# Sums of squares per head: one fp32 matmul against two rounded passes, in a hybrid attention / DeltaNet layer

## The chip, the core and the metric

The kernel runs on one core of one Trainium2 chip. The metric is the device time in microseconds of one execution. TensorE (PE) multiplies, VectorE (DVE) and ScalarE (ACT) do the elementwise work, GpSimd (POOL) clears a few tiles and issues some DMAs, SyncE (SP) issues most DMAs.

## The reference

One layer over 512 latent tokens and 256 context tokens of width 1024. Two mixers run side by side: windowed attention with normalised queries and keys, and a gated DeltaNet whose queries and keys are normalised too. Their outputs are gated, projected and added; a squared-ReLU MLP follows. What matters here are the two normalisations, both over the 64 features of one head:

```python
def rms_norm(x, g):
    xf = x.astype(jnp.float32)
    return xf * lax.rsqrt(jnp.mean(xf * xf, axis=-1, keepdims=True) + EPS) * g.astype(jnp.float32)

def l2_normalize(x):
    return x * lax.rsqrt(jnp.sum(x * x, axis=-1, keepdims=True) + EPS)
...
q_a = axial_rope(rms_norm(heads(aq, ATTN_Q_HEADS), q_norm_g), row, col)
k_a = axial_rope(rms_norm(heads(ak, ATTN_KV_HEADS), k_norm_g), row, col)
k_ac = rms_norm(heads(cak, ATTN_KV_HEADS), k_norm_g)
...
q_d = l2_normalize(heads(q_d, DN_HEADS)) * DN_HEAD_DIM ** -0.5
k_d = l2_normalize(heads(k_d, DN_HEADS))
```

## The kernel before, in words

Features lie on partitions and tokens on columns, so one tile of 128 partitions holds two heads. A sum over the 64 features of a head is a sum over 64 partitions. The kernel takes it on PE: `bones` is a 128x128 matrix of ones in two diagonal blocks of 64, and `bones` times the squares gives on each partition the sum of its own head.

The large projections are not run in plain fp32. A value is split into an upper part `hi` (ACT rounds it to the short format fp32r, L224) and a rest `lo` (DVE subtracts, L225), and `mm3` (L331, L333, L335) adds the products upper-upper, upper-rest and rest-upper in the same PSUM bank. Weights are split in the same manner (`wh` on ACT, L295; `wl` on DVE, L300, or by a DMA that GpSimd issues, L297 and L298). The sums of squares are the exception: `bones` and the squares are plain fp32 and go in one matmul call, which the trace shows as two MATMUL records.

There are 13 such sums of 512 columns and 5 of 256:

- `qk_norm` (the matmul is L566): attention keys, 512 latent columns and 256 context columns; four tiles of attention queries, 512 columns each. ACT squares the projection (L563) and copies it with its gain (L564), PE sums, DVE rotates (L569 to L572), ACT takes Ln and Exp of the sums (L185, the line of a helper), DVE multiplies (L577).
- `l2n` (L781): four tiles of DeltaNet keys, 512 and 256 columns each (in the order of the program just before `chunk_mats`); four tiles of DeltaNet queries of 512 columns, beside the first steps of the scan. ACT squares (L778), PE sums, ACT takes Ln and Exp, DVE multiplies (L786, L788).

A further matmul with `bones` (L861) sums decays and is of 96 columns.

Around these sums the program goes on as follows. `chunk_mats` builds the decay matrices (L913 to L939), `invert` solves triangular systems on DVE in a long row of small dependent steps (L972, L973), first for the context, later for the latent chunks. `back` (L983) transposes the results, `combine` (L993 to L1004) and the scan steps (`chain_step`, L1243 to L1322) use them on PE. Attention runs between (`scores`, reduction on DVE at L681; `outputs`, L725 to L747). Projections of gates (L1148, L1194) are work for PE that nothing waits for at once.

Buffers in SBUF come from a ring of 167 units of 256 columns (`Arena`): `alloc` takes the next free place behind the last one, `free` gives it back; large tiles that stay are taken from the far end. `NSKIP` moves the ring's pointer on at one place, by as many turns of `alloc(1024).free()`, four units each.

The order of instructions on each engine is not the order of the program. A planner (`Lists.run`) gives each instruction a cost and a latency, and lets each engine take the ready instruction of lowest rank. Ranks are positions in the program, moved by the table `SHIFTS` (an engine or all, a first and an end position, so many places). The order it finds is fixed in the program that runs.

Of the kernel before, what the change touches and what calls it, by code (L numbers as in the profile page):

```python
# [10 lines left out]
F32 = mybir.dt.float32  # L11
F32R = mybir.dt.float32r
BF16 = mybir.dt.bfloat16
AF = mybir.ActivationFunctionType
# [20 lines left out]
NPL = ()  # L35
WEARLY = 0
STICK = 50
NSKIP = 2
WARM = (0, 3, 3, 3, 2, 0, 0, 0)
NROWS = 2  # L40
ND1 = 3
# [1 line left out]
P = 128  # L43
# [74 lines left out]
def tile_layer(ctx: ExitStack, tc: tile.TileContext, I: dict, out: bass.AP, dbg=None):  # L118
    nc = tc.nc
    V, A, G, PE = nc.vector, nc.scalar, nc.gpsimd, nc.tensor  # L120
# [5 lines left out]
    mats = ctx.enter_context(tc.tile_pool(name="mats", bufs=1))  # L126
# [16 lines left out]
    alloc, bank = mem.get, lambda n=1: banks.get(n * 512)  # L143
# [3 lines left out]
    def load(out, key, *at):  # L147
        d = nc.sync.dma_start(out=out, in_=I[key][at] if at else I[key])
        if lastload:
            tie(d.ins, lastload[0].ins.name)  # L150
        return d

    def cload(key, shape, pool=const):
        t = pool.tile(list(shape), F32, name=f"c_{key}")
        load(t, key)
        return t
# [5 lines left out]
    r32 = lambda ap: ap.bitcast(F32R)  # L162
# [14 lines left out]
    def act(out_, in_, func, **kw):  # L177

        sets = TABLES.get(func)
        if sets and actg["set"] not in sets:  # L180
            head = A.preload_act_table_set(sets[0])
            for o in actg["ops"]:
                tie(head.ins, o.name)
            actg.update(set=sets[0], head=head.ins, ops=[head.ins])
        r = A.activation(out_, in_, func, **kw)  # L185
        if sets:
            tie(r.ins, actg["head"].name)
            actg["ops"].append(r.ins)
        return r
# [255 lines left out]


    ident = cload("ident", [P, P], mats)
    bones = cload("bones", [P, P], mats)
    identb = mats.tile([P, P], BF16, name="identb")
    V.tensor_copy(identb, ident)  # L450
    maskb = mats.tile([P, 2, P], BF16, name="maskb")
# [3 lines left out]
    mt.free()  # L455
    cs = alloc(1024, True)
    cost, sint = cs[:, :512], cs[:, 512:]
    load(cost, "cost")
    load(sint, "sint")
    selq = cload("selq", [64, 80])  # L460
# [37 lines left out]

    for _ in range(NSKIP):
        alloc(1024).free()  # L500
# [55 lines left out]
                return e.value  # L556


    def qk_norm(acc, n, gain, turn=False):

        t = alloc(1024)
        raw, sq = t[:, :n], t[:, 512:512 + n]
        A.activation(sq, acc, AF.Square)  # L563
        A.activation(raw, acc, AF.Copy, scale=gain)  # L564
        ss = bank()
        PE.matmul(ss[:, :n], bones, sq, start=True, stop=True)  # L566
        if turn:
            rot = alloc(512)
            V.stream_shuffle(rot.ap, raw, [(i + 16) % 32 for i in range(32)])  # L569
            V.tensor_tensor(raw, raw, cost, op=ALU.mult)  # L570
            V.tensor_tensor(rot.ap, rot.ap, sint, op=ALU.mult)
            V.tensor_tensor(raw, raw, rot.ap, op=ALU.add)  # L572
            rot.free()
        act(sq, ss[:, :n], AF.Ln, bias=epsc, scale=1.0 / HD)
        ss.free()
        act(sq, sq, AF.Exp, scale=-0.5)
        V.tensor_tensor(raw, raw, sq, op=ALU.mult)  # L577
        return t
# [13 lines left out]
    def k_attn():  # L592

        acc = yield from in_tile_steps(T_AK, True)
        t = qk_norm(acc[:, :512], SEQ, kg, True)
        t2 = qk_norm(acc[:, 512:768], CTX, kg)
        acc.free()
        for src, o in ((t[:, :512], slice(0, 512)), (t2[:, :CTX], slice(512, 768))):
            for kv, r in enumerate(own):
                for r2 in own:  # L600
                    A.activation(r32(KH[kv][r2, o]), src[r], AF.Copy)
                V.tensor_tensor(r32(KLo[kv][r, o]), src[r], KH[kv][r, o], op=ALU.subtract)
        t.free()
        t2.free()
        yield
# [19 lines left out]
    def q_attn(j):  # L625
        acc = yield from in_tile_steps(T_AQ + j, False)
        t = qk_norm(acc.ap, SEQ, qgs, True)
        acc.free()
        src = t[:, :512].rearrange("p (b t) -> p b t", b=4)
        for kv, r in enumerate(own):  # L630
            split(src[r], Q[kv][r, :, j, :], Q[kv][own[1 - kv], :, j, :])
        t.free()
        yield
# [140 lines left out]
    def l2n(y, scale, parts, eps):  # L774

        n = parts[-1][1]
        t = alloc(n)
        A.activation(t.ap, y, AF.Square)  # L778
        for lo, hi in parts:
            ss = bank()  # L780
            PE.matmul(ss[:, :hi - lo], bones, t[:, lo:hi], start=True, stop=True)  # L781
            act(t[:, lo:hi], ss[:, :hi - lo], AF.Ln, bias=eps)
            ss.free()
        act(t.ap, t.ap, AF.Exp, scale=-0.5)
        if scale == 1.0:
            V.tensor_tensor(y, y, t.ap, op=ALU.mult)  # L786
        else:
            V.scalar_tensor_tensor(y, y, scale, t.ap, op0=ALU.mult, op1=ALU.mult)  # L788
        t.free()
# [10 lines left out]
    t, t2 = alloc(TOK), alloc(TOK)  # L800
# [249 lines left out]
    def mats():  # L1050
        for q in range(4):
            l2n(kT[q].ap, 1.0, ((0, SEQ), (SEQ, TOK)), epsc)
            yield
        for gi in range(3):
            yield from chunk_mats(gi)
# [282 lines left out]
    def rest():  # L1338
        for q in range(4):
            l2n(qT[q].ap, HD ** -0.5, ((0, SEQ),), epsc4)  # L1340
            yield
        for g in (1, 2):
            to_tokens(VTM, vT, g)
            yield
        for t in vT:
            t.free()
        for g in (1, 2):
            to_tokens(KTM, kT, g)
            yield
# [30 lines left out]
    for g in range(2):  # L1380
# [20 lines left out]
        for a in range(2):  # L1401
            lo, hi = quad(a, 0), quad(a, 1)
# [38 lines left out]
    for qq in range(2):  # L1441
# [3 lines left out]
        for a in range(2):  # L1445
            n = 2 * qq + a
            t = alloc(512)
# [304 lines left out]
class Step:  # L1752
# [39 lines left out]
    def cost(self):  # L1792

        n = self.cols
        if self.kind == "InstMatmult":
            if self.dtype.endswith("32r"):
                return (226 if n == 512 else max(60, 7 + .44 * n)), n * .44 + 175
            if self.dtype.endswith("16"):
                return 96, 240
            if self.whole:  # L1800
                return (110, 280) if self.ins.is_transpose else (max(62, 1.72 * n), max(62, 1.72 * n) + 170)
            return (142, 300) if self.tile[0] == P else (30 if self.tile[1] > HC else 19, 220)
        if self.kind == "InstStreamTranspose":
            return 1950, 2090
        if self.eng == "DVE":
            own = 67 + 1.04 * n + 60 * self.psum if n > 8 else 100
            return own, own + 85
        if self.eng == "Activation":
            own = 1290 if "Load" in self.kind else max(195, 36 + .893 * n) + 20 * self.psum
            return own, own + 130  # L1810
        return 550, 560


# [67 lines left out]
class Lists:  # L1881
# [114 lines left out]


SHIFTS = (
# [12 lines left out]
)  # L2011


# [120 lines left out]
```

## Time and profile before

| what | us |
|---|---|
| median of 3 runs | 871.12 (870.12 to 871.73) |
| profiled execution, its own time | 871.5 |
| its span in the trace | 869.7 |
| PE busy | 852.3 |
| DVE busy | 647.0 |
| ACT busy | 498.4 |

The span is the time from the first to the last instruction in the trace; 1.8 us of the profiled execution's time lie around it. Busy is time in which at least one instruction of the engine is under way. The granted clock of PE is full in every slice.

### The profile page before, as it was taken

What the parts mean: (1) busy time and instruction counts of PE and PEld (TensorE: products, weight loads), DVE (VectorE), ACT (ScalarE), POOL (GpSimd) and SP (SyncE); (2) the same over time, 40 slices, a digit from 0 to 9 for tenths busy, and PEclk for the clock granted to TensorE, in tenths of its full rate; (3) what the DMA queues carried; (4) which work ended last, traced back from release to release, by engine and by line L of the source; (5) the groups of instructions that cost most, each with busy time, mean ns of one, the idle gap of its engine ahead of it and who ended that gap; (6) DMA issues with size and microseconds to landing.
All of it is one profiled execution on the core that took longest, in us unless ns stands there. A gap on an engine that the chain in (4) does not pass through costs nothing.

```text
span 869.7 us, 17973 instructions
## 1 busy us (share of the span) xinstructions
PE 852.3 (98%) x7544; PEld 712.8 (82%) x7544; DVE 647.0 (74%) x1113; ACT 498.4 (57%) x882; POOL 26.1 (3%) x42
## 2 busy tenths in 40 slices
PE   9999999999999999899999999999999999999998
PEld 6688778877777778677778899888998899889986
DVE  4865899987779997867848969993876478648741
ACT  5567875487669886587754435552555256415620
POOL 0000001010000002000000000000000000000000
PEclk9999999999999999999999999999999999999999
DMA  9924465533121236733116744743412332342031
GB/s 365 352 72 98 88 134 122 120 76 70 38 38 31 68 131 212 243 99 100 40 54 220 264 144 131 249 139 121 146 33 74 122 140 70 97 128 92 26 121 49
DMA packets 31986, 106.86 MB, mean 123 GB/s; under 512 B 4001, under 2 KB 4513, under 8 KB 31905
## 3 DMA queue, kind: packets, MB, share of 16 engines
q1 hardware_dynamic: 29600, 97.33, 33.6%
q0 software_dynamic: 2304, 8.39, 6.2%
q8 instruction: 59, 0.97, 0.5%
q14 instruction: 23, 0.18, 0.1%
HBM read 103.61 MB, written 2.10 MB: 122 GB/s over the span
## 4 chain that ended last, share of the span: by engine, by line
PE 77%; DVE 9%; ACT 6%; DMA 6%; issue 2%; SPq 0%; ACTq 0%; DVEq 0%
PE banks L331 14%; PE banks L333 14%; PE banks L335 14%; PE banks L1612 14%; PE banks L1148 7%; DMA m<-in_wada 3%; PE banks L1243 3%; PE banks L1194 3%; ACT m L185 2%; PE banks L725 1%; DVE wl L300 1%; DMA wr<-in_win 1%; PE banks L781 1%; DVE m L511 1%; DMA wr<-in_wbr 1%
## 5 line engine op out<-in xcount | busy, mean ns | idle before, releaser
L331 PE MATMUL banks<-m,wh 128*128 128x512 f32 (+1 forms) x568 | 210.7, 374 | 2.2 <-ACT m L224 1.3
L333 PE MATMUL banks<-m,wh 128*128 128x512 f32 (+1 forms) x568 | 211.2, 372 | 0.0
L335 PE MATMUL banks<-m,wl 128*128 128x512 f32 (+1 forms) x568 | 209.9, 370 | 0.1
L295 ACT ACTIVATE wh<-wr 128x1024 fp32r<-128x1024 f32 (+1 forms) x92 | 90.4, 984 | 128.3 <-PE banks L333 82.7
L331 PEld LDWEIGHTS banks<-m,wh 128*128 128x128 f32 x568 | 107.0, 189 | 20.4 <-ACT m L224 1.5
L1612 PEld LDWEIGHTS banks<-m,m 128*128 128x128 f32 x1008 | 122.2, 192 | 0.7
L335 PEld LDWEIGHTS banks<-m,wl 128*128 128x128 f32 x568 | 106.9, 188 | 19.2 <-issue 1.0
L1612 PE MATMUL banks<-m,m 128*128 128x256 f32 x1008 | 122.4, 283 | 0.0
L333 PEld LDWEIGHTS banks<-m,wh 128*128 128x128 f32 x568 | 107.1, 188 | 18.1 <-issue 0.7
L224 ACT ACTIVATE m<-m 128x512 fp32r<-128x512 f32 (+2 forms) x118 | 82.4, 721 | 66.1 <-PE banks L1612 14.9
L1148 PE MATMUL banks<-m,wh 128*128 128x512 f32 x320 | 104.1, 402 | 1.8 <-ACT m L185 1.0
L225 DVE TENSOR_TENSOR m<-m,m 128x512 fp32r<-128x512 f32 (+2 forms) x118 | 92.3, 804 | 15.5 <-ACT m L224 13.9
L300 DVE TENSOR_TENSOR wl<-wr,wh 128x1024 fp32r<-128x1024 f32 (+1 forms) x76 | 84.3, 1109 | 17.1 <-ACT wh L295 14.6
L1739 DVE SCALAR_TENSOR_TENSOR m<-banks,modT,m 128x512 f32<-128x512 f32 x32 | 24.0, 749 | 65.0 <-PE banks L335 64.9
L1148 PEld LDWEIGHTS banks<-m,wh 128*128 128x128 f32 x320 | 58.6, 188 | 14.4 <-ACT m L185 1.4
L1148 PE MATMUL banks<-m,wl 128*128 128x512 f32 x160 | 63.7, 400 | 0.4 <-DVE wl L300 0.4
L331 PE MATMUL banks<-m,m 128*128 128x256 f32 (+1 forms) x136 | 45.5, 340 | 0.4 <-ACT m L295 0.3
L333 PE MATMUL banks<-m,m 128*128 128x256 f32 (+1 forms) x136 | 45.6, 342 | 0.1
L511 DVE SCALAR_TENSOR_TENSOR m<-m,m 128x1024 f32<-128x1024 f32 x32 | 39.1, 1222 | 8.4 <-DMA m<-in_wada 8.2
L335 PE MATMUL banks<-m,m 128*128 128x256 f32 (+1 forms) x120 | 40.2, 337 | 0.0
L1243 PEld LDWEIGHTS banks<-m,m 64*64 64x64 f32 x1600 | 26.7, 134 | 12.5 <-issue 4.3
L1148 PEld LDWEIGHTS banks<-m,wl 128*128 128x128 f32 x160 | 30.0, 188 | 7.3 <-DVE wl L300 1.1
(263 smaller groups left out, 1313.7 us busy)
## 6 DMA issues: line engine op xcount, KB each, us to landing
m<-in_wada SPq DMA_DIRECT2D x48, 512.0 KB, 4.8
wr<-in_wm SPq DMA_DIRECT2D x40, 512.0 KB, 3.6
wr<-in_win SPq DMA_DIRECT2D x38, 512.0 KB, 3.7
m<-in_wm SPq DMA_DIRECT2D x24, 512.0 KB, 3.7
wl<-in_win POOLq DMA_DIRECT2D x16, 512.0 KB, 5.8
m<-in_xT SPq DMA_DIRECT2D x8, 512.0 KB, 5.9
wr<-in_wbr SPq DMA_DIRECT2D x16, 256.0 KB, 2.7
wr<-in_wout SPq DMA_DIRECT2D x8, 512.0 KB, 4.4
```

The lines of the kernel that those rows point to most:

```text
L224: A.activation(r32(hi), src, AF.Copy)
L225: (eng or V).tensor_tensor(r32(lo), src, hi, op=ALU.subtract)
L295: upper[0] = A.activation(r32(hi), raw, AF.Copy)
L300: V.tensor_tensor(r32(lo), raw, hi, op=ALU.subtract)
L331: PE.matmul(acc, w[0][:, k, :], xhi, start=(start and i == 0), stop=False)
L333: r = PE.matmul(acc, w[0][:, k, :], xlo, start=False, stop=(end and w[1] is None))
L335: r = PE.matmul(acc, w[1][:, k, :], xhi, start=False, stop=end)
L511: r = V.scalar_tensor_tensor(wa.ap, wa.ap, 0.5, scr_[0].ap, op0=ALU.mult, op1=ALU.mult, accum_out=modT[:, grp, j:j + 1])
L1148: PE.matmul(acc.ap, w[x][:, k, :], hx[k][y], start=(k == p == 0), stop=(k == KT - 1 and p == 2))
L1194: PE.matmul(pa.ap, w[x][:, j, :], r32(Q[y][:, :, j, :]), start=(j == p == 0), stop=(j == 3 and p == 2))
L1243: runs[n].append(PE.matmul(out_, w, x, start=True, stop=True).ins.name)
L1612: PE.matmul(dst, r32(self.w[w][i][:, k * P:(k + 1) * P]), xs7[x][k][j], start=(n == 0), stop=(n == 11))
```

## The change

Three things change.

1. Each of the 18 sums of squares goes in two passes. A new helper takes two buffers from the ring, lets ACT round the squares into the first and DVE subtract them into the second (`split`), and adds two fp32r matmuls with `bones` in one bank. `bones` itself is loaded into a buffer of the ring and copied into its place by ACT, so that it is marked as rounded; it holds only ones and zeros. The sum of the decays (L861) stays in fp32.
2. The ring's pointer is moved by seven turns in place of two.
3. `SHIFTS` is another table, of 69 entries in place of 60. The planner also gets a cost for a subtraction on GpSimd, which is not used: `POOLS` is False, and the subtraction is on DVE.

```diff
-NSKIP = 2
+NSKIP = 7
+POOLS = False
...
-    bones = cload("bones", [P, P], mats)
+    bones = mats.tile([P, P], F32, name="bones")
+    bt = alloc(256)
+    load(bt[:, :P], "bones")
+    A.activation(r32(bones), bt[:, :P], AF.Copy)
+    bt.free()
+    SPLITTER = G if POOLS else V
...
+    def ones_sum(dst, sq):
+
+        n = sq.shape[-1]
+        hi, lo = alloc(n), alloc(n)
+        split(sq, hi.ap, lo.ap, SPLITTER)
+        PE.matmul(dst, r32(bones), r32(hi.ap), start=True, stop=False)
+        PE.matmul(dst, r32(bones), r32(lo.ap), start=False, stop=True)
+        hi.free()
+        lo.free()
+
     def qk_norm(acc, n, gain, turn=False):
...
-        PE.matmul(ss[:, :n], bones, sq, start=True, stop=True)
+        ones_sum(ss[:, :n], sq)
...
-            PE.matmul(ss[:, :hi - lo], bones, t[:, lo:hi], start=True, stop=True)
+            ones_sum(ss[:, :hi - lo], t[:, lo:hi])
...
+        if self.kind == "InstTensorTensor":
+            return 100 + 2.2 * n, 200 + 2.2 * n
         return 550, 560
...
 SHIFTS = (
-    (0, 2729, 2759, -37), (0, 7350, 8025, -10), (-1, 4917, 4924, 10), (0, 1436, 2436, 180), (-1, 5117, 5177, 30),
...
+    (0, 5262, 5282, 10), (4, 85, 205, 80), (0, 2465, 2615, -30), (2, 7546, 7946, 1000), (2, 6238, 6638, -200),
...
 )
```

24 rows, old and new, of the table SHIFTS are left out of this document.

## The prediction

> **What bounds the kernel now.** I read the page first: the busy times and the chain of work that ended last.
>
> ```profile
> span 869.7 us, 17973 instructions
> PE 852.3 (98%) x7544; PEld 712.8 (82%) x7544; DVE 647.0 (74%) x1113; ACT 498.4 (57%) x882; POOL 26.1 (3%) x42
> ...
> PE 77%; DVE 9%; ACT 6%; DMA 6%; issue 2%; SPq 0%; ACTq 0%; DVEq 0%
> ```
>
> PE is busy for 852.3 of 869.7 us and idle for 17.4 us in all, and 77% of the last chain are its instructions. What shortens PE's work shortens the run, as long as the rest of the order keeps PE fed. An average over the whole says nothing of the places where the sums stand, so I asked next for the busy time by stretches (start and end, length, then busy time and count for each engine, granted clock, DMA share, GB/s). The sums run from 74 to 131 us (keys of both mixers, attention queries) and from 283 to 298 us (DeltaNet queries).
>
> ```profile
> 66.00:99.00 33.00, 20.79 (x41) 1.00 0.42 88
> ...
> 99.00:189.00 90.00, 88.42 (x754) 71.19 (x752) 85.99 (x165) 55.88 (x92) 9.87 (x13) 1.00 0.54 115
> 189.00:281.00 92.00, 88.36 (x689) 70.24 (x688) 72.89 (x131) 69.87 (x127) 3.46 (x4) 1.00 0.22 47
> 281.00:335.00 54.00, 54.00 (x681) 41.08 (x679) 52.66 (x94) 47.95 (x106) 2.07 (x4) 1.00 0.33 103
> 335.00:380.00 45.00, 41.73 (x844) 32.90 (x842) 33.72 (x59) 27.74 (x53) 6.24 (x12) 1.00 0.61 207
> ```
>
> The first line is DVE alone; in the others the columns after the length are PE, weight load, DVE, ACT, POOL. Two things are to be seen. PE is idle for 1.6, 3.6, 0.0 and 3.3 us in the four later stretches, 8.5 us together. And DVE, which is to get 18 new subtractions, is free for 12.2 of 33 us between 66 and 99 and for 19.1 of 92 us between 189 and 281, but full from 99 to 189 (4.0 of 90 us free) and from 281 to 335 (1.3 of 54 us free). Both engines are full where two thirds of the sums stand: the change moves work from one to the other.
>
> **What PE saves.** The chain of waits gives the pitch of matmuls on PE, since there each piece lasts from one release to the next (start, length, what).
>
> ```profile
> 69.57 0.12 PE banks L333
> ...
> 70.04 0.23 PE banks L333
> ...
> 74.00 1.29 PE banks L781 x4
> ...
> 122.52 0.87 PE banks L566 x2
> ...
> 130.33 0.86 PE banks L566 x2
> ```
>
> An fp32r matmul of 512 columns takes 0.23 us of PE, one of 256 takes 0.12. A key tile's two fp32 sums, 512 and 256 columns, take 1.29 us in four records; a sum of 512 columns alone takes 0.86. In two passes these become 2 x 0.23 + 2 x 0.12 = 0.70 and 2 x 0.23 = 0.46 us. The savings are 0.59 us for each of five key tiles (one of attention, four of DeltaNet) and 0.40 us for each of eight query tiles: 2.95 + 3.20 = 6.2 us (6.15 before rounding). The number of weight loads stays at two for each sum.
>
> The Trainium skill (FP8 and Floating Point Precision, TensorE Precision Notes) has a true fp32 product as four passes through the array. By that a sum of 512 columns would cost 0.92 us, not the 0.86 of the row, and the saving would come out near 7.1 us; I keep the row.
>
> **What is added on DVE and ACT.** Subtractions and rounding copies of this form stand in the trace already (mean ns of one before the second bar); for their pitch I take neighbours on a full DVE (start, length).
>
> ```profile
> L225 DVE TENSOR_TENSOR m<-m,m 128x512 fp32r<-128x512 f32 x84 | 56.3, 687 | 9.7 <-ACT m L224 8.3 <-PE banks L1612 0.8
> ...
> 108.38 0.69 DVE L572 TENSOR_TENSOR m<-m,m 128x512 f32<-128x512 f32 x1
> 108.98 0.69 DVE L929 TENSOR_TENSOR m<-m,m 128x512 f32<-128x512 f32 x1
> ...
> 361.53 0.42 DVE L1395 TENSOR_TENSOR m<-m,banks 128x256 f32<-128x256 f32 x1
> 361.86 0.69 DVE L1153 SCALAR_TENSOR_TENSOR m<-m,m 128x512 f32<-128x512 f32 x1
> ```
>
> ```profile
> L224 ACT ACTIVATE m<-m 128x512 fp32r<-128x512 f32 x84 | 51.7, 627 | 57.3 <-PE banks L1612 14.9 <-DMA m<-in_wm 13.4 <-DVE m L1470 6.4
> ```
>
> On DVE a subtraction of 512 columns costs 0.60 us from start to start and one of 256 columns 0.33 us: 13 x 0.60 + 5 x 0.33 = 9.5 us in all. Of these the DeltaNet keys take 4 x 0.93 = 3.7 us, the attention keys and queries 0.93 + 4 x 0.60 = 3.3 us, the DeltaNet queries 4 x 0.60 = 2.4 us. On ACT a rounding copy of 512 columns lasts 0.63 us, and one of 256 is bounded by the same, so the 18 copies are at most 18 x 0.63 = 11.3 us.
>
> What hides them: for the DeltaNet keys, the 12.2 us in which DVE is free between 66 and 99 us; they cost nothing, and 3.7 us on DVE's queue if that cover is gone. ACT is busy for 57% of the whole span, for 55.9 of 90 us in the first full stretch of DVE and for 48.0 of 54 us in the second; there four more copies (2.5 us) still fit into its 6 us. I cost ACT at nothing but the wait below. The subtractions of the attention tiles (3.3 us) and of the DeltaNet queries (2.4 us) lie in the two full stretches and have no cover there. They push back what stands behind them on DVE. What that is in the second stretch is seen in its order of time:
>
> ```profile
> 320.66 0.21 DVE L973 TENSOR_TENSOR m<-m,m 128x60 f32<-128x60 f32 x1
> ...
> 321.36 2.02 DVE L983 STREAM_TRANSPOSE m<-m 128x1024 f32<-128x1024 f32 x1
> ```
>
> The last step of the second inversion ends at 320.9 us, the transposes of its result follow, and `combine` and the latent scan wait for them. PE has gate projections to run meanwhile (it has no idle time from 281 to 335), so a shift of 2.4 us moves filler forward and costs PE time only where filler runs short. In the first stretch the same holds for the first inversion and the attention scores; behind it come 19.1 us of free DVE time in which 3.3 us can be made up.
>
> **The new wait.** Between the squares and the sum now stand two instructions on two engines. The first pass waits for ACT, the second for DVE. PE works its queue in order, so if a sum stands too early, everything behind it on PE stands too, and Ln, Exp and the product come later by the same. The nearest row is the wait that the sums have today for their squares (total us, times, longest):
>
> ```profile
> PE banks L566 <- ACT m L563: 1.0, 2, 0.6
> ```
>
> Five tiles bring 1.0 us of such waits, in two of them, both behind a full ACT. The change can cost nothing here (the planner puts other matmuls ahead of the sum) or this much again for each of the two added producers on the attention tiles, 2.0 us. I take the row itself once more, 1.0 us, as the price of both, the new wait and the fuller DVE: it is the only place where this trace shows PE standing for a sum of squares. The bounds are 0 and, if both full stretches of DVE pass their subtractions on to PE, 3.3 + 2.4 = 5.7 us.
>
> **What goes at nothing.** The load of `bones` now goes through a buffer of the ring and a copy on ACT.
>
> ```profile
> L781 PE MATMUL banks<-m,c_bones x24: 379/592/627, 73.8 to 297.8; 128*128 128x512 f32 x16, 128*128 128x256 f32 x8
> ...
> L148 SPq DMA_DIRECT2D c_bones<-in_bones x1: 423/423/423, 31.7 to 31.7; - x1
> ...
> DMA to landing us min/median/max: 7.4/7.4/7.4
> ```
>
> It is issued at 31.7 and has landed at 39.1 us, and its first use is at 73.8 us: 34.7 us of cover for a copy that is bounded by 0.63 us. If the new buffer were late, weight loads behind it on SP's queue would be late too; the masks go through a ring buffer right behind it already. The five more turns of the ring use no engine; they and the 18 pairs of buffers change which old users a later buffer waits for.
>
> **The new order.** No row shows what the new table does. What it can win back is part of PE's 8.5 us of idle time in the four stretches; what it can lose is as much. I take zero for it, and plus or minus half, 4.2 us, for the range.
>
> **The sum.** 871.5 - 6.2 + 1.0 = 866.3 us against the profiled execution; the median is 0.4 us below that execution, so 865.9 us. A measurement can tell about 0.2% from no change, 1.7 us; the forecast is 0.6% faster.
>
> **Rivals.**
>
> DVE takes over as the bound (slower). Place: the full stretches from 99 and from 281 us, with the DeltaNet keys' sums ahead of them. For it: DVE is busy 96% and 98% there, and its work there ends in the transposes that the scan needs. Against it: 19.1 us of free DVE time between the stretches, and PE never idle from 281 to 335. If all 9.5 us of subtractions come back as PE idle time, the run takes 871.1 - 6.2 + 9.5 = 874.4 us. It decides for slower once PE's idle time from 66 to 380 us grows by more than 6.2 + 1.7 = 7.9 us. Chance 0.18, with a bad new order counted in.
>
> PE is not the bound although it is busy (same). Then the 6.2 us turn into idle time in front of the instructions that already set the pace, such as the scan's steps: 871.1 us. For it: 23% of the last chain are not PE. Against it: the pitches of 0.23 and 0.12 us stand as two to one, as the columns do, so PE is streaming, not waiting, inside its busy time. Chance 0.08. The Trainium skill (Trainium Kernel Development and Optimization, Best Practices) would have the distance to the limit judged by the busy share of weight loads, not by that of matmuls; here that is 82%, not 98%, which would leave 18% of slack on PE and speaks for this rival. The trace speaks against it by the pitches above.
>
> The new order wins more. The 1.0 us isn't paid and half of the 8.5 us goes: 871.1 - 6.2 - 4.2 = 860.7 us. For it: the idle time exists, and shorter sums free their banks earlier. Against it: DVE is fuller than before. Chance 0.12.
>
> That the change doesn't do what it says has little room: the matmul in fp32r with 512 columns is the kernel's most frequent one, at a pitch that every stretch shows.
>
> **How the numbers follow.** The forecast gets 0.62. Its own range is 863.8 us (half of the order's 4.2 us won) to 868.8 us (half of the 5.7 us lost). Faster by over 0.2% is the forecast and the third rival, 0.74; same is the second, 0.08; slower is the first, 0.18. For 8 in 10 the range goes down to 861.5, which takes in half of the third rival, and up to 872.0, which takes in the second and the mild part of the first.
>
> **What would show it.** Right: the 18 sums stand in the trace as 36 fp32r matmuls with mean durations near those of other fp32r matmuls; PE's busy time falls by about 6 us, to 846; DVE's rises by about 10 us; PE's idle time from 66 to 380 us stays within 2 us of 8.5; the time of the later stretches, from 380 us on, is only moved, not changed. Wrong: PE's busy time falls as said, and its idle time rises by as much, in front of matmuls that wait for DVE, behind 99 us (scores, values) or behind 321 us (combine, scan); or the second inversion ends later than 321 us. If the stretch behind 380 us changes its length by more than 2 us, it is the new table that did it, which I can't forecast.

## The result and the profile after

| | us |
|---|---|
| before, beside the changed kernel | 871.23 (870.12 to 871.73) |
| after | 880.79 (877.36 to 881.23) |
| ratio | 1.0103, interval 1.0076 to 1.013 |
| profiled execution of after, its span | 881.23, 879.5 |

The kernel became 1.0% slower. The forecast was 865.9 us, 0.6% faster, with a range up to 872.0. In the changed file the lines have moved: L331, L333 and L335 are L332, L334 and L336; the helper of ACT is L186, the split is L225 (ACT) and L226 (DVE); the gate projection is L1164, `combine` L1019 and L1020, the half products of `chunk_mats` L910, the transposes in `back` L999. The two passes are L570 (upper part) and L571 (rest).

From the page of after, the span, the busy times and the granted clock in 40 slices:

```profile
span 879.5 us, 18035 instructions
PE 855.7 (97%) x7544; PEld 715.4 (81%) x7544; DVE 658.7 (75%) x1131; ACT 504.7 (57%) x901; POOL 26.0 (3%) x42
...
PEclk9999999999999999899999999999999999999999
```

The counts are as expected: 7544 matmul records, 18 more instructions on DVE, 19 more on ACT. But PE's busy time rose by 3.4 us where it was to fall by 6, its idle time rose from 17.4 to 23.8 us, and one slice of the clock isn't full. The stretches of the prediction, in after (start and end, length, PE, weight load, DVE, ACT, POOL, granted clock, DMA share, GB/s):

```profile
66.00:99.00 33.00, 32.96 (x333) 27.09 (x332) 23.89 (x48) 30.38 (x53) 2.73 (x3) 1.00 0.46 97
99.00:189.00 90.00, 88.02 (x692) 70.69 (x691) 87.87 (x171) 56.45 (x93) 8.80 (x11) 1.00 0.52 113
189.00:281.00 92.00, 85.59 (x727) 67.55 (x727) 70.03 (x126) 68.28 (x126) 4.49 (x6) 1.00 0.21 45
281.00:335.00 54.00, 52.62 (x531) 40.05 (x530) 49.92 (x96) 45.99 (x106) 0.00 (x0) 1.00 0.28 83
335.00:380.00 45.00, 40.94 (x971) 32.44 (x973) 36.26 (x56) 26.22 (x46) 7.25 (x14) 0.92 0.62 205
```

PE is idle for 2.0, 6.4, 1.4 and 4.1 us in the four later stretches, 13.8 us in all against 8.5. Half of what is new (2.8 us) stands from 189 to 281 us, where no sum of squares stands and DVE is free for 22 us. What PE waits for in the whole run (total us, times, longest):

```profile
PE banks L1164 <- ACT m L186: 3.2, 3, 1.4
PE banks L1019 <- issue: 2.9, 1, 2.9
PE banks L741 <- ACT m L186: 1.6, 3, 0.9
PE banks L334 <- DVE m L342: 1.3, 4, 0.7
...
PE banks L570 <- ACT m L225: 0.5, 1, 0.5
PE banks L570 <- ACT m L1052: 0.4, 1, 0.4
```

The wait at the sums, the one that the change adds, is 0.9 us, about the 1.0 us that it was priced at. The larger ones are gate projections and attention outputs (L741) that wait for ACT, and one gap of 2.9 us inside `combine` that the view puts down to no releaser ("issue"; the last section has its cause). The passes themselves, groups by shape (busy us, mean ns, then idle time before them):

```profile
L571 PE MATMUL banks<-m,bones 128*128 128x512 f32 x13 | 5.6, 427 | 0.0
L570 PE MATMUL banks<-m,bones 128*128 128x512 f32 x13 | 5.5, 423 | 0.9 <-ACT m L225 0.5 <-ACT m L1052 0.4
L570 PE MATMUL banks<-m,bones 128*128 128x256 f32 x5 | 1.5, 302 | 0.0
L571 PE MATMUL banks<-m,bones 128*128 128x256 f32 x5 | 1.4, 280 | 0.0
```

There are the 36 short matmuls. Finally two places further down, in order of time on DVE (the end of the second inversion) and on PE (the last matmuls of `combine`, and the first of the MLP):

```profile
332.78 0.11 DVE L994 MEMSET m<- 128x64 f32 x1
332.93 2.17 DVE L999 STREAM_TRANSPOSE m<-m 128x1024 f32<-128x1024 f32 x1
```

```profile
360.38 0.29 PE L1020 MATMUL banks<-m,m 32*32 32x32 f32 x2
...
622.94 0.52 PE L1628 MATMUL banks<-m,m 128*128 128x256 f32 x3
```

In before the same places in PE's order stand as follows:

```profile
350.79 0.19 PE L1004 MATMUL banks<-m,m 32*32 32x32 f32 x1
...
614.02 0.64 PE L1612 MATMUL banks<-m,m 128*128 128x256 f32 x4
```

The transposes of the inversion start 11.6 us later than before, `combine` ends 9.7 us later, and the MLP starts 8.9 us later. So nearly all of the 9.8 us of span is lost ahead of the MLP.

**Where the time went.** Summing, for each matmul, the time from the end of the matmul before it to its own end, without the idle time in it, gives what each kind of matmul costs PE. By that account the way from 869.7 to 879.5 us is:

| | before to after, us |
|---|---|
| the sums of squares, 13.9 to 8.9 | -5.0 |
| PE idle, from its first matmul to its last | +6.4 |
| one stretch at half clock (below) | +2.7 |
| the other matmuls, the same ones, at a longer pitch | +5.7 |
| span | +9.8 |

The saving is there. What outweighs it is in the three other lines, of which the prediction had only 1.0 us, as idle time. Two parts of them belong to this execution: 1.1 us of the longer pitch lie in the first 7 us (last section), and the half clock doesn't stand in every execution. After's four have mean granted clocks of 0.996, 0.998, 1.000 and 1.000, and the two at 1.000 took 880.58 and 877.36 us, still above every run of before beside them. Three things were changed at once, so the trace alone can't say which of them brought the rest.

### The profile page after: what moved, and what is told of

Read it like the earlier page. It is cut to its first block, busy times and chain, and to the rows that moved or that the text cites. A ratio compares the mean times of both kernels' runs of the same rounds, so it can differ in the third digit from the quotient of the medians.

```text
span 879.5 us, 18035 instructions
## 1 busy us (share of the span) xinstructions
PE 855.7 (97%) x7544; PEld 715.4 (81%) x7544; DVE 658.7 (75%) x1131; ACT 504.7 (57%) x901; POOL 26.0 (3%) x42
## 5 line engine op out<-in xcount | busy, mean ns | idle before, releaser
L332 PE MATMUL banks<-m,wh 128*128 128x512 f32 (+1 forms) x568 | 210.9, 373 | 2.7 <-DVE m L763 1.0
L334 PE MATMUL banks<-m,wh 128*128 128x512 f32 (+1 forms) x568 | 209.3, 371 | 0.0
L336 PE MATMUL banks<-m,wl 128*128 128x512 f32 (+1 forms) x568 | 208.8, 370 | 0.0
L225 ACT ACTIVATE m<-m 128x512 fp32r<-128x512 f32 (+3 forms) x136 | 91.8, 700 | 72.8 <-DMA m<-in_wm 13.8
L332 PEld LDWEIGHTS banks<-m,wh 128*128 128x128 f32 x568 | 107.0, 188 | 21.3 <-ACT m L186 1.7
L226 DVE TENSOR_TENSOR m<-m,m 128x512 fp32r<-128x512 f32 (+3 forms) x136 | 104.0, 778 | 25.0 <-ACT m L225 23.1
L336 PEld LDWEIGHTS banks<-m,wl 128*128 128x128 f32 x568 | 106.8, 188 | 17.7
L334 PEld LDWEIGHTS banks<-m,wh 128*128 128x128 f32 x568 | 106.9, 188 | 16.9
L1164 PE MATMUL banks<-m,wh 128*128 128x512 f32 x320 | 106.0, 406 | 3.4 <-ACT m L186 3.2
L1164 PEld LDWEIGHTS banks<-m,wh 128*128 128x128 f32 x320 | 60.0, 191 | 17.0 <-ACT m L186 4.2
L1164 PE MATMUL banks<-m,wl 128*128 128x512 f32 x160 | 65.2, 408 | 0.4 <-DVE wl L301 0.4
L334 PE MATMUL banks<-m,m 128*128 128x256 f32 (+1 forms) x136 | 44.8, 341 | 1.3 <-DVE m L342 1.3
L332 PE MATMUL banks<-m,m 128*128 128x512 f32 (+1 forms) x136 | 44.7, 341 | 0.9 <-ACT m L341 0.5
L336 PE MATMUL banks<-m,m 128*128 128x512 f32 (+1 forms) x120 | 38.5, 333 | 0.0
L1164 PEld LDWEIGHTS banks<-m,wl 128*128 128x128 f32 x160 | 30.6, 191 | 7.1 <-DVE wl L301 0.9
```

What stands on the lines that cost most here:

```text
L225: A.activation(r32(hi), src, AF.Copy)
L226: (eng or V).tensor_tensor(r32(lo), src, hi, op=ALU.subtract)
L332: PE.matmul(acc, w[0][:, k, :], xhi, start=(start and i == 0), stop=False)
L334: r = PE.matmul(acc, w[0][:, k, :], xlo, start=False, stop=(end and w[1] is None))
L336: r = PE.matmul(acc, w[1][:, k, :], xhi, start=False, stop=end)
L1164: PE.matmul(acc.ap, w[x][:, k, :], hx[k][y], start=(k == p == 0), stop=(k == KT - 1 and p == 2))
```

## The experiments

Theory A: the passes pay about as forecast, and the new order (the table, with the ring's new place) is what loses. Theory B, the first rival of the prediction: the subtractions on DVE and the added waits cost more than the passes save. All ratios are against the kernel before, run beside the experiment; that one had a median of 871.8 to 872.3 us in these comparisons.

**The old sums in the new order.** After's fixed order, ring and buffers are kept; each sum is again one fp32 matmul, with no copy and no subtraction.

```diff
-        split(sq, hi.ap, lo.ap, SPLITTER)
-        PE.matmul(dst, r32(bones), r32(hi.ap), start=True, stop=False)
-        PE.matmul(dst, r32(bones), r32(lo.ap), start=False, stop=True)
+        PE.matmul(dst, bones, sq, start=True, stop=True)
```

> The changed kernel's order and ring kept instruction for instruction, but each sum again one fp32 matmul on the squares (no rounding copy, no subtraction; the ring's two buffers are still taken and given back). Theory A, the new order is what costs the time and the two passes pay: PE's work rises by about 5 us and the run is 2 to 5 us slower than the changed kernel's 880.8, so 883 to 886 us. Theory B, the subtractions and the waits they bring cost more than the passes save: the run is faster than the changed kernel, 871 to 877 us.

Measured: 882.71 us, ratio 1.0132 (1.0111 to 1.0153), just below A's band and far above B's. This kernel does the work of before, with before's sums (and one small copy of `bones` on ACT), and is 10.9 us slower. Its page, and its waits of PE:

```profile
span 880.9 us, 18001 instructions
PE 858.2 (97%) x7544; PEld 714.9 (81%) x7544; DVE 649.9 (74%) x1113; ACT 496.8 (56%) x883; POOL 26.0 (3%) x42
```

```profile
PE banks L1162 <- ACT m L186: 5.2, 4, 2.3
```

DVE has its old 1113 instructions, and PE stands as in after, in front of the gate projections (L1162 here). The account of PE shows the same lines as in after, without the passes: idle time +5.3 us, the other matmuls +5.6 us, the sums +0.3 us. The second inversion ends even later:

```profile
336.32 0.11 DVE L992 MEMSET m<- 128x64 f32 x1
```

The prediction had named a late inversion as the mark of subtractions on a full DVE. Here it is late with none. So the order alone, with the ring's place, can cost this much; that an order made for two passes is merely unfit for one isn't ruled out by this run, and the better table further down decides that. From this kernel to after the sums give 5.4 us, of which 1.1 us go into idle time and 2.7 us into the half clock, which this profiled execution doesn't have; in two others of its five the clock is at 0.996 as in after's profile, and they took 885.0 and 885.4 us against after's 881.2. By the medians the passes are worth about 2 us in this order, by like clocks 3 to 4 us, and the two ratios' intervals overlap.

**The subtractions left out.** After's order is kept; the second pass reads the upper part again, so the rest is not added and the sums are twice the rounded squares' sums.

```diff
-        split(sq, hi.ap, lo.ap, SPLITTER)
+        A.activation(r32(hi.ap), sq, AF.Copy)
         PE.matmul(dst, r32(bones), r32(hi.ap), start=True, stop=False)
-        PE.matmul(dst, r32(bones), r32(lo.ap), start=False, stop=True)
+        PE.matmul(dst, r32(bones), r32(hi.ap), start=False, stop=True)
```

> The changed kernel's order and ring kept, but the 18 subtractions are left out and the second pass reads the upper part again, so the sums are not the reference's; PE's work is that of the changed kernel, and VectorE is relieved of about 10 us. Theory A: within 2 us of the changed kernel's 880.8, since VectorE's queue is not what costs the time. Theory B: 4 to 9 us faster, 872 to 877 us.

Measured: 877.92 us, ratio 1.0068 (1.0053 to 1.0082), 2.9 us below after by the medians, between the bands of A and B. The interval overlaps after's (1.0076 to 1.013), so A's 2 us aren't excluded. The profiled spans are 2.8 us apart: 0.9 us is the gap in `combine`, here 2.0 us, and 1.0 us is the half clock, here for 3.4 us. Nothing shows that these two come from the subtractions; the other 0.9 us may. B needs more than 2.9 us: 6 us are still missing to before without any subtraction.

**The two ways in other tables.** After and before, each with another `SHIFTS`.

```diff
-SHIFTS = (...)   # after: 69 entries; before: 60
+SHIFTS = (...)   # after: 51 others; before: 87 others
```

> The changed kernel with another table of 89 shifts, found by a longer search with the kernel's own planner; sums, ring and everything else as in the changed kernel. Theory A: the loss goes with the table; 862 to 870 us, below the kernel before. Theory B: the loss stays with the sums; 874 us or more.

> The kernel before with another table of 90 shifts, from a search of the same length as that of the two-pass kernel beside it. Control for the search: what a longer search alone is worth. Theory A: 866 to 871 us, and the two-pass kernel with its searched table is 2 to 5 us below this one. Theory B: this one is below the two-pass kernel with its searched table.

Measured: 903.70 us, ratio 1.0363 (1.0346 to 1.038), and 917.28 us, ratio 1.0519 (1.0496 to 1.0541). A failed in both. The first time lies in B's "874 us or more", but the second one is above the first, where B had it below. Neither decides anything, for a reason of mine: some shifts in these tables were broken by an overflow of the numbers, so the orders in the program were not the ones that the expectations spoke of, nor are the entry counts. As two arbitrary orders they still say one thing: the same work, with the same sums as before, takes 871 or 917 us by its order alone.

**The passes put into the old order by hand.** Before's order of instructions, with copies, subtractions and second passes put in at their place in it; `NSKIP` is 2, and the pairs of buffers are taken from the far end, so that the ring turns as before.

```diff
-NSKIP = 7
+NSKIP = 2
...
-        hi, lo = alloc(n), alloc(n)
+        hi, lo = alloc(n, True), alloc(n, True)
```

> Two-pass sums in the order of the kernel before, instruction for instruction: the ring's pointer is moved by two turns as before, the sums' buffers are taken from the ring's far end so that all other buffers stay where they were; each rounding copy stands on ScalarE's queue right behind the squares that it reads, each subtraction on VectorE's queue where that copy stood in the old plan's order, both passes where the one matmul stood. Theory A, the order is the loss and the two passes pay about 2 us net of the subtractions: 867 to 871 us, at or below the kernel before's 871.8. Theory B, the passes lose wherever VectorE is full: 873 to 880 us.

Measured: 897.83 us, ratio 1.0303 (1.0289 to 1.0317). Both theories failed, by over 15 us. The waits of PE:

```profile
PE banks L571 <- DVE m L226: 6.0, 8, 3.2
PE banks L570 <- ACT m L225: 4.9, 8, 1.4
PE banks L1047 <- DVE m L491: 2.7, 1, 2.7
PE banks L910 <- DVE m L955: 2.1, 2, 1.1
```

In an order made for one matmul per sum, the new waits cost 10.9 us at the sums alone, against 0.9 us in after's. So the 1.0 us of the prediction isn't a property of the change; it holds where the order has put other matmuls ahead of the sums. So a change that adds producers is hard to take apart from a new order; no other placement in the old order was run.

**No table at all.** `SHIFTS` is empty, in after and in before; everything else is kept.

```diff
+SHIFTS = ()
```

> The changed kernel with an empty table: the planner's order untouched. Theory A: the table of the changed kernel was worth little on the chip, so this one is within 1.5% of it, 880 to 893 us, and it is no slower than the one-pass kernel with an empty table beside it. Theory B: it is slower than that one by 4 us or more.

> The kernel before with an empty table. Theory A: 882 to 895 us, that is, the old table is worth more than 10 us on the chip, more than the new one is worth to the changed kernel. Theory B: 876 to 886 us, below the two-pass kernel with an empty table.

Measured: 892.14 us, ratio 1.0232 (1.0218 to 1.0246) with two passes; 888.47 us, ratio 1.0195 (1.0172 to 1.0218) with one. Both times lie in A's bands. In the planner's bare order two passes are 3.7 us slower, where A had them no slower and B 4 us or more. The intervals touch, and the profiled executions lose 6.8 us (two passes) and 1.7 us (one) to half clock, so this difference is no price of the passes. The old table is worth 16.5 us to the kernel with one pass (888.5 to 872.0), the new one 11.3 us to the kernel with two (892.1 to 880.8). The new table is the weaker of the two.

**A better table for each.** After with a table of 61 entries, and before with one of 59 entries sought in the same way; then the first one's order with the old sums in it; and a two-pass kernel with the old place of the ring (`NSKIP = 2`, buffers from the far end) and its own table of 66 entries.

```diff
-SHIFTS = (...)   # after: 69 entries
+SHIFTS = (...)   # 61 others
```

> The changed kernel with another table (61 shifts), searched so that the order the kernel's planner makes of it also holds when costs vary by 5% and PE's clock halves after a stretch with PE half idle. Sums and ring as in the changed kernel. Theory A, the loss is the order's alone: 862 to 869 us, faster than the kernel before. Theory B, the two passes lose wherever they stand: 874 us or more.

> The kernel before with another table (59 shifts) from the same search at the same length. It is the control for the two-pass kernel beside it. Theory A: 864 to 870 us, 1 to 3 us slower than the two-pass kernel beside it. Theory B: faster than that one by 3 us or more.

> The order of the two-pass kernel of this call, kept instruction for instruction, with each sum again one fp32 matmul and no rounding copy or subtraction (as in the first experiment, in a second order). Theory A: slower than that two-pass kernel by 2 to 5 us. Theory B: faster than it by 1 us or more.

> Two-pass sums with the ring of the kernel before (two turns, the sums' buffers from the far end) and a table from the same search (66 shifts). If the ring's place matters less than the order, as theory A has it: within 4 us of the two-pass kernel of this call, 864 to 872 us. If the old ring is what the kernel before lived on: faster than that one by 3 us or more. Theory B: 874 us or more.

| | us | ratio to before, interval |
|---|---|---|
| two passes, better table | 872.31 | 0.9994 (0.998 to 1.0009) |
| one pass, table sought likewise | 877.01 | 1.0046 (1.003 to 1.0062) |
| one pass in the first one's order | 877.43 | 1.0058 (1.0039 to 1.0078) |
| two passes, ring as before | 876.86 | 1.0048 (1.003 to 1.0065) |

The two-pass kernel with another table is 8.5 us faster than after by the medians of the two comparisons (1.1% by their ratios), with the same ring and not one arithmetic instruction changed, and as fast as before. So it is the table that loses; A's 862 to 869 us wasn't reached, B's 874 or more isn't met either. In its order the old sums cost 5.1 us more by the medians, just above the 2 to 5 us that A expected. The tables sought in the same way give two passes 4.7 us over one, more than A's 1 to 3 us, and the one-pass kernel lies above A's 864 to 870 us. Both comparisons may favour two passes: the first order was made for them, and the second search, with one pass, stayed behind the old table. Against the old table with one pass, the best such kernel here, two passes win nothing. There is no sign that before lives on the ring's old place: with it the two-pass kernel is 4.6 us slower than with the new one. That is outside A's 4 us and 864 to 872 us and inside B's 874 us or more, and the two differ in their tables as well.

From the page of the two-pass kernel with the better table, and from that of the old sums in its order:

```profile
span 871.4 us, 18027 instructions
PE 850.9 (98%) x7544; PEld 715.4 (82%) x7544; DVE 654.2 (75%) x1131; ACT 506.8 (58%) x901; POOL 26.1 (3%) x42
```

```profile
PE 856.3 (98%) x7544; PEld 716.3 (82%) x7544; DVE 646.1 (74%) x1113; ACT 499.0 (57%) x883; POOL 26.1 (3%) x42
```

PE is busy for 5.4 us less with two passes. The account of PE says the same of the sums, 13.6 to 8.3 us. Its idle time is 1.7 us larger, so these two spans are 3.7 us apart. From before to the two-pass kernel the account has -5.6 us for the sums, +3.2 for idle time, +1.7 for a stretch at half clock and +2.5 for the other matmuls (1.2 of it at the start), +1.7 us in all.

## Why the prediction was wrong

**The saving: right.** Forecast 6.2 us, measured 5.0 us in after and 5.6 us in the better order. The term is 1.2 us too large in after because 26 passes of 512 columns were priced at 0.23 us, the pitch inside a long row of such matmuls; by the account each costs about 0.29 us in after, where the two stand between other lines; the old sums were priced at 13.3 us and cost 13.9 us, which takes back a part. The prediction's second price, by four passes, comes to 7.2 us and not to 7.1 us, and lies further off.

**The new wait and the fuller DVE: right in the sum, not as a property.** Forecast -6.2 + 1.0 = -5.2 us for the passes with all they bring. In the better order they are worth 5.1 us, by the medians. That this is so near is in part luck: the two profiled spans give 3.7 us. In after's order 2 to 4 us are left; put into the old order by hand, the waits at the sums alone cost 10.9 us. The bounds of 0 to 5.7 us didn't hold what an unfit order does.

**The new order: the step that failed.** "No row shows what the new table does. [...] I take zero for it, and plus or minus half, 4.2 us, for the range." With the old sums in it, after's order is 10.9 us slower than before's, and with another table in the same ring after's work is 8.5 us faster. The bound was drawn from PE's idle time in four stretches (8.5 us), as if an order could lose no more than there was to win. An order has no such bound on its slow side: one of the experiments lost 45 us by order alone. No row of before gives that size, and the range should have been open to the slow side for it.

**PE's idle time: half of the story.** The prediction had the slow side decide once the idle time from 66 to 380 us grew by more than 7.9 us. It grew by 5.3 us, under that point, and the kernel was slower all the same. The test left out that a busy PE can be a slower one: 2.7 us at half clock and 5.7 us of longer pitch (1.1 us of it at the start) count as busy.

**The late inversion: right sign, other cause.** The inversion's transposes start at 332.9 us where the prediction gave 321 us as the mark of DVE as the new bound. The first experiment has it at 336 us with no subtraction. A mark that a second cause can leave too shows neither.

**The stretch behind 380 us.** The test was to tell of the table, but it cuts at a time, not at a piece of work, and all the work had moved. Counted from the MLP's first matmul to the end, the run has 255.7 us before and 256.6 us after, so the table's loss stands ahead of it.

**At nothing.** The load of `bones` and the DeltaNet keys' subtractions were right: PE has no idle time from 66 to 99 us (0.04 us in all). For ACT's copies no run here has a price alone; the waits of gate projections for ACT aren't theirs, since they are 5.2 us without the copies and 3.2 us with them.

**Rivals.** "DVE takes over" had the sign and "a bad new order counted in", at 0.18; its mechanism, its place and its 874.4 us were not what happened. "PE is not the bound" fell: in one order 5.4 us less on PE gave 5.1 us by the medians, 3.7 us between the profiled spans.

What stays open: which entries of the new table lose; why the same matmuls take 5.7 us more in after's order (1.1 us is the start, below; 1.5 us are the half products, whose 384 of the first part stand from 87.4 to 124.9 us between other work, before from 91.5 to 117.1; the rest is in pieces of 1.0 us or less); and whether an order exists in which two passes beat the kernel before. None of the orders run here does.

## What to carry to other kernels

When a change comes with a schedule found anew, price the two apart: run the old work in the new order, and the new work in an order sought with equal care, before saying anything of the work itself. A bound for an unknown order isn't the idle time that is there to win; it goes far to the slow side, and waits that a good order hides in 1 us cost 11 us in an unfit one. A saving on the bounding engine is read from that engine's busy time in one and the same order, where it came out within 1 us of the forecast; an order made for one of the two kernels may favour it.

## What the runs showed of the hardware

**A half-idle window is enough to halve PE's clock.** In after the clock is at half for 6.8 us. The stretch ahead of it and the stretch itself (columns as above):

```profile
354.60:358.00 3.40, 1.60 (x58) 0.96 (x56) 2.97 (x4) 2.93 (x6) 0.28 (x1) 0.99 0.84 284
358.00:364.80 6.80, 5.41 (x85) 4.48 (x86) 1.42 (x3) 2.55 (x5) 3.10 (x6) 0.50 0.77 262
```

PE was idle for 1.8 of 3.4 us, 1.5 us of it inside the one gap in `combine`, and the clock fell. It was busy for 5.4 us at half speed, so 2.7 us were lost to a gap of 2.9 us: the gap cost nearly twice its length. The better order has the same at another place, in front of an attention matmul:

```profile
194.40:197.80 3.40, 1.04 (x6) 0.68 (x5) 0.43 (x2) 2.77 (x7) 0.00 (x0) 1.00 0.47 93
197.80:201.20 3.40, 3.40 (x17) 2.90 (x16) 0.98 (x2) 1.71 (x3) 0.00 (x0) 0.50 0.02 5
```

The stretches at half clock last one, two or three times 3.41 us in all thirteen traces, but for the one that ends each. Cutting each trace into windows of that length, set by where its clock changes, all in which PE was idle for 0.54 of the time or more were followed by half clock, none below 0.50 was that started from full clock, and between the two both occur. Once at half clock, it stayed there behind windows with 0.33 to 0.57 idle, and once with 0.12; it came back to full behind windows with 0.13 or less. It is the idle share of the window that counts, not one long gap: in the two-pass kernel without a table a longest gap of 1.3 us was enough. In before's profiled execution no window reaches 0.4, and it lost nothing in this way. Others of its executions did: of the 22 beside the better tables, those at a mean clock of 1.000 took 870.7 to 872.2 us, those at 0.995 and 0.996 took 874.1 to 874.5 us. The Trainium skill (TensorE: Matmul & The Clock Gate, Part 1: The HAM clock gate) has a free-running window of 3413 ns, and the half rate after at least one idle window; the window's length agrees, but here one half idle was enough.

**PE waits for its own instructions.** The gap in `combine`, behind a row of 32x32 matmuls, is put down to "issue": 2.9 us in after, 1.2 us at the same lines in before. The trace shows what ends it. Among the DMA queues of after one carries instructions (packets, MB, share):

```profile
q8 instruction: 59, 0.97, 0.4%
```

Its 59 packets of 16384 bytes fit PE's own queue, whose 7544 matmuls and 7544 weight loads are 59 blocks of 256. In the thirteen traces 19 idle gaps of PE over 0.7 us are put down to "issue". Each ends 1.2 to 1.6 us after one of these packets has landed, and each at the same place in a block of 256 instructions. In after the packet is under way from 357.18 to 358.11 us, and PE goes on at 359.39 us. In before the packet starts 1.6 us ahead of the gap, in after 0.7 us into it; why, the traces don't show. The page's share of "issue" doesn't show such a gap in advance, and by the window above it weighs more than its length.

**The start.** In the same 2.2 us near the start PE ran 22 matmuls in before and 13 in after, of the same kind. First before, then after:

```profile
4.20:6.40 2.20, 2.20 (x22) 2.20 (x21) 0.69 (x1) 1.82 (x2) 0.00 (x0) 1.00 0.96 361
```

```profile
4.20:6.40 2.20, 2.20 (x13) 2.20 (x12) 0.14 (x1) 0.42 (x2) 0.00 (x0) 1.00 1.03 391
```

That is 1.1 us of after's longer pitch, with no cause in the change. The clock records of the traces begin with full clock at 4.16 us in before and at 6.39 us in after; ahead of the first record the view counts the clock as full, so its column reads 1.00 in both. In the thirteen traces the first record stands between 4.16 and 7.14 us, so before's profiled execution had the earliest start of all. The same page of the Trainium skill has the warm-up vary from run to run, by where the first matmul falls in the window; the rows and the records agree.
